# Expert stage of a two-block network: low halves of the weights on VectorE, all dense gates through DRAM, own buffers for the gathered rows

## The chip, the core and the metric

The kernel runs on one core of one Trainium2 chip. The metric is the device time of one execution in microseconds. Three timed runs of the kernel before gave 3890.19, 3895.22 and 3896.65 us; their median, 3895.22 us, is the number to beat or to match.

## The reference, cut to what matters

A DiT-like two-layer network is followed by a second block (gated delta rule beside a linear recurrence, attention over a memory) and, as its last part, a product-key expert layer on 512 tokens of 1024 features. The change touches only that last part:

```python
def peer_ffn(h, wq, subkeys, u_tab, v_tab):      # u_tab, v_tab: 16384 experts x 1024
    q = (t @ wq).reshape(ntok, 8, 2, 128)         # 8 heads, two half keys
    sc = einsum('thpd,hpkd->thpk', q, subkeys)    # 128 sub-keys for each half
    s1, i1 = top_k(sc[:, :, 0], 16)
    s2, i2 = top_k(sc[:, :, 1], 16)
    cand = s1[..., :, None] + s2[..., None, :]
    best, pos = top_k(cand.reshape(ntok, 8, 256), 16)
    idx = e1 * 128 + e2                           # place of an expert in the 128 x 128 grid
    gate = softmax(best, axis=-1)
    # for each token: 8 x 16 experts
    act = gelu(einsum('phkd,pd->phk', u_tab[ib], tb)) * gb
    return einsum('phk,phkd->pd', act, v_tab[ib])
```

The output is the RMS-normalised sum of the stream and this layer, in float32.

## The kernel before, in words

Matrix products take float32 operands as a sum of two parts in the fast float32 format: a high half and a low half (the rest). `mm3` (L274) forms each product from three matmuls: high by high, high by low, low by high. `weight` (L264) loads a weight tile of 128 x 1024 (512 KB) into a buffer `wr`, lets ScalarE write the high half `wh` (L245) and another engine write the low half `wl` by a subtraction (L253). That engine is GpSimd, except where the call says `'dve'`.

The expert layer (`peer`, L1384) treats its four tiles of 128 tokens in two ways. Three tiles ("dense") go through all 16384 experts in 128 blocks: `hidden(b)` (L1418) multiplies block b of the u table (8 products of three matmuls, 128 x 384 outputs, `H`), applies gelu (`Hg`); `operand` (L1463) multiplies the result with the gates of that block and splits it into `ach` and `acl`; then 18 matmuls of 512 columns (L1541) add its product with block b of the v table to six PSUM banks `acc`, which stay for all 128 blocks. The fourth tile ("fetched") reads only the experts that its tokens chose: 128 steps `up` (an indirect DMA of 128 rows, 512 KB, of the u table, and one VectorE instruction, L1562, that takes their dot products) and 128 steps `down` (the same for the v table; L1573 adds the weighted rows to `y0`). The gathers are issued by GpSimd (L1557). `fetches(n)` puts n further steps into the program; the calls spread them over the blocks.

The layer runs in four stages. (1) Scores and `topk`. (2) `decode` (L1684) turns positions into rows, columns and gates with one-hot tables `oh` of 128 x 1024; `gates` (L1602) expands them to dense gates: for every 4 tokens VectorE and ScalarE write two one-hot tables `o`, TensorE multiplies them into `G`, and ScalarE copies the result to `Gs` (two buffers of 4 MB, for 64 tokens each). Tiles 0 and 1 of the dense ones are then written to DRAM (`dGate`); those of the last tile stay in `Gs`. Meanwhile `hidden` runs for the first 72 blocks, whose results go to DRAM (`dAct`). (3) Blocks 0 to 71: each reads its `Hr` back from `dAct`, and for every two blocks the gates `Gt` from `dGate` (rows of 512 bytes); VectorE multiplies by `Gt` (L1470) and twice by `Gs` (L1473). This stretch is called the head below. (4) Blocks 72 to 127, which compute `hidden` here: the tail. Of the v weights two in three have their low half on GpSimd, one in three on VectorE (L1530); the u weights have theirs on GpSimd.

Weights, gathered rows and some results share the 7 buffers `wr`. The order of each engine's instructions isn't that of the source: the framework's scheduler sets it when the program is built, from a model of each instruction's time and from when buffers come free. Once built, the order is fixed, and each engine takes its instructions in that order; SyncE issues all plain DMAs in order, GpSimd the gathers in order.

## Time and profile before

| | |
|---|---|
| timed runs, us | 3890.19, 3895.22, 3896.65 |
| profiled execution, span first to last instruction, us | 3892.8 |
| busy share of the span | PE 91%, DVE 73%, POOL 52%, ACT 39% |
| first one-hot table of `decode` | 2597 us |
| first dense gates (`Gs`) to the last | 2698 to 2992 us |
| first matmul into `acc` | 3003.7 us |
| end of the head, first product of block 72 | about 3340 us |
| last matmul into `acc` | 3881 us |

The profile has one time for the profiled execution, its span, 2.4 us under the median of the timed runs. In its rows PE is TensorE, PEld its weight loads, DVE VectorE, ACT ScalarE, POOL GpSimd, SP SyncE. Consecutive matmuls overlap in the records, so the distance between their starts, not their duration, is what one costs. PEclk is the clock that TensorE was granted, as a share of full speed. The DMA share is the mean busy share of the 16 DMA engines. All stages before 2597 us are other parts of the network.

### The profile page before, as it was taken

Reading aid. Unit: us, or ns where it says so; the run is one execution under the profiler, and the core shown is the slowest. Engines: PE = TensorE matmul, PEld = TensorE weight load, DVE = VectorE, ACT = ScalarE, POOL = GpSimd, SP = SyncE. Lnnn points to the kernel's source line nnn. Section 1 sums busy time; section 2 is a strip of 40 time slices with the busy share of each in tenths; the row PEclk is TensorE's granted clock in tenths of the full one; section 3 lists DMA queues with packets and bytes.
Section 4 is the critical chain, followed back from the end, with each engine's and each line's share of the span. In section 5 each row is a group of like instructions: output and inputs, shape, how many; then the busy total and the mean of one; then the engine's idle time right before and its main releaser. Section 6 shows DMA issues by size and latency. Waiting matters only on the chain.

```text
span 3892.8 us, 51884 instructions
## 1 busy us (share of the span) xinstructions
PE 3539.8 (91%) x18415; PEld 2940.5 (76%) x18415; DVE 2841.6 (73%) x5128; ACT 1536.0 (39%) x2548; POOL 2004.9 (52%) x1230
## 2 busy tenths in 40 slices
PE   6899898999999869999999998997799999989898
PEld 4566666788877767788787976897788777777777
DVE  7895768778779793322486354789998999888874
ACT  4433663332323343322344443343576233322223
POOL 3763105345555553344445432467545676888773
PEclk9999998999999889999999998998999999999999
DMA  5442023344434343223322333245576998888782
GB/s 215 141 145 66 25 69 101 107 131 126 131 99 157 124 182 119 86 93 98 120 76 89 110 116 107 84 139 179 181 248 214 316 319 306 283 284 290 274 285 90
DMA packets 279012, 615.42 MB, mean 158 GB/s; under 512 B 49888, under 2 KB 148832, under 8 KB 275936
## 3 DMA queue, kind: packets, MB, share of 16 engines
q1 hardware_dynamic: 237248, 477.34, 37.3%
q0 software_dynamic: 36864, 134.23, 10.0%
q8 instruction: 145, 2.38, 0.3%
q10 hardware_dynamic: 4640, 0.53, 0.1%
q14 instruction: 115, 0.94, 0.1%
HBM read 539.27 MB, written 72.71 MB: 157 GB/s over the span
## 4 chain that ended last, share of the span: by engine, by line
PE 21%; DVE 9%; POOL 8%; issue 7%; DMA 4%; ACT 1%; POOLq 0%; ACTq 0%; DVEq 0%; SPq 0%
POOL wl L253 4%; POOL wr L1557 3%; PE mm L277 3%; PE mm L279 3%; PE mm L278 3%; DMA wr<-in_p_v_dram,idx 2%; PE H L279 2%; PE H L278 2%; PE H L277 2%; DVE o L1617 1%; PE acc L279 1%; PE acc L277 1%; PE acc L278 1%; PE G L1620 1%; DVE wr L1562 1%
## 5 line engine op out<-in xcount | busy, mean ns | idle before, releaser
L253 POOL TENSOR_TENSOR wl<-wr,wh 128x1024 fp32r<-128x1024 f32 x469 | 1168.7, 2495 | 1043.3 <-ACT wh L245 975.2
L245 ACT ACTIVATE wh<-wr 128x1024 fp32r<-128x1024 f32 x512 | 536.2, 1053 | 690.7 <-PE mm L278 352.4
L277 PE MATMUL mm<-hh,wh 128*128 128x512 f32 (+1 forms) x1024 | 365.6, 363 | 17.7 <-ACT hh L340 8.0
L279 PE MATMUL H<-wh,wl 128*128 128x384 f32 x1024 | 352.8, 344 | 18.8 <-POOL wl L253 17.6
L278 PE MATMUL mm<-hl,wh 128*128 128x512 f32 (+1 forms) x1024 | 366.8, 359 | 0.1
L279 PE MATMUL mm<-hh,wl 128*128 128x512 f32 (+1 forms) x1024 | 363.9, 356 | 0.9 <-POOL wl L253 0.8
L277 PE MATMUL H<-wh,wh 128*128 128x384 f32 x1024 | 348.9, 341 | 1.5 <-ACT Hg L1425 1.5
L278 PE MATMUL H<-wl,wh 128*128 128x384 f32 x1024 | 349.5, 341 | 0.0
L277 PE MATMUL acc<-wh,ach 128*128 128x512 f32 x768 | 310.0, 404 | 26.4 <-ACT ach L245 24.9
L279 PE MATMUL acc<-wh,acl 128*128 128x512 f32 x768 | 308.9, 406 | 19.1 <-DVE acl L253 19.0
L278 PE MATMUL acc<-wl,ach 128*128 128x512 f32 x768 | 306.8, 399 | 0.0
L277 PE MATMUL mm<-fh,wh 128*128 128x512 f32 (+1 forms) x768 | 276.6, 361 | 2.2 <-DVE x L531 2.2
L278 PE MATMUL mm<-fl,wh 128*128 128x512 f32 (+1 forms) x768 | 275.9, 360 | 2.4 <-DVE fl L253 2.4
L279 PE MATMUL mm<-fh,wl 128*128 128x512 f32 (+1 forms) x768 | 274.8, 359 | 0.0
L1573 DVE SCALAR_TENSOR_TENSOR y<-wr,wgt,y 128x1024 f32<-128x1024 f32 x127 | 230.0, 1811 | 50.3 <-DMA wr<-in_p_v_dram,idx 49.8
L277 PEld LDWEIGHTS mm<-hh,wh 128*128 128x128 f32 x1024 | 197.9, 194 | 52.6 <-ACT hh L340 9.2
L1562 DVE SCALAR_TENSOR_TENSOR wr<-wr,tt 128x1024 f32<-128x1024 f32 x128 | 206.0, 1616 | 40.8 <-DMA wr<-in_p_u_dram,idx 23.4
L279 PEld LDWEIGHTS mm<-hh,wl 128*128 128x128 f32 x1024 | 197.8, 193 | 29.5 <-POOL wl L253 1.7
L278 PEld LDWEIGHTS mm<-hl,wh 128*128 128x128 f32 x1024 | 198.4, 194 | 28.1 <-issue 0.9
L1557 POOL DMA_INDIRECT wr<-in_p_u_dram,idx x128 | 162.4, 1269 | 107.3 <-DVE wr L1562 48.5
L279 PEld LDWEIGHTS H<-wh,wl 128*128 128x128 f32 x1024 | 195.1, 191 | 29.1 <-POOL wl L253 28.7
L1557 POOL DMA_INDIRECT wr<-in_p_v_dram,idx x128 | 167.9, 1312 | 93.6 <-DVE y L1573 46.2
(809 smaller groups left out, 8754.5 us busy)
## 6 DMA issues: line engine op xcount, KB each, us to landing
wr<-in_mlp_w_dram SPq DMA_DIRECT2D x128, 512.0 KB
wr<-in_p_ut_dram SPq DMA_DIRECT2D x128, 512.0 KB
wr<-in_p_v_dram SPq DMA_DIRECT2D x128, 512.0 KB
aw<-in_ada_w_dram SPq DMA_DIRECT2D x48, 512.0 KB
wr<-in_ada_w_dram SPq DMA_DIRECT2D x32, 512.0 KB
dGate<-Gs SPq DMA_DIRECT2D x32, 512.0 KB
Gt<-dGate SPq DMA_DIRECT2D x64, 256.0 KB
dAct<-Hg SPq DMA_DIRECT2D x72, 192.0 KB
```

The lines of the kernel that those rows point to most:

```text
L245: self.nc.scalar.activation(dst, src, AF.Copy, **({} if scale is None else {'scale': scale}))
L253: e.tensor_tensor(dst, src, hi.bitcast(F32), op=OP.subtract)
L277: mm(out, ah, bh, start=first, stop=False)
L278: mm(out, ah, bl, start=False, stop=False)
L279: mm(out, al, bh, start=False, stop=last)
L1557: gp.indirect_dma_start(out=r, out_offset=None, in_=tab, in_offset=bass.IndirectOffsetOnAxis(ap=idx[:, s:s + 1], axis=0))
L1562: v.scalar_tensor_tensor(r, r, 1.0, tt, op0=OP.mult, op1=OP.mult, accum_out=dots[:, s:s + 1])
L1573: v.scalar_tensor_tensor(y0, r, wgt[:, s:s + 1], y0, op0=OP.mult, op1=OP.add)
L1617: v.tensor_scalar(o1[:, t], iota, row, gate, op0=OP.is_equal, op1=OP.mult)
L1620: nc.tensor.matmul(p[:, t * 128:(t + 1) * 128], o2[:, t], o1[:, t], start=True, stop=True)
```

## The change

The low halves: `weight` takes its engine from a new field, `'pool'` at first and `'dve'` from the end of `topk` on, so that all 256 weight tiles of stages 2 to 4 have their low half on VectorE; so has the multiplication of the one-hot tables in `decode`. The gates: all three dense tiles are written to DRAM, read back four blocks at a time (rows of 1 KB, 768 KB for each read), and one VectorE instruction multiplies a whole block. The 8 MB of `Gs` are given back after stage 2. The gathered rows: in stages 3 and 4 they have 9 buffers of their own (`rw`), and the 7 `wr` are left to the weights.

```diff
+        self.lo_eng = 'pool'
...
-    def weight(self, ap, lo_eng='pool'):
+    def weight(self, ap, lo_eng=None):
+        lo_eng = lo_eng or self.lo_eng
...
+            self.rp, self.rb_ = self.wp, ('wr', self.wb[0])
...
-            dG = tc.dram_tile([ND - 1, 2, 128, 128, 64], F32, name='dGate')
+            dG = tc.dram_tile([ND, 2, 128, 128, 64], F32, name='dGate')
...
-            G2 = [self.t(gp_, [128, 128, 64], f'Gs{i}') for i in range(2)]
             with ExitStack() as e1:
+                G2p = e1.enter_context(self.pool('pgs'))
+                G2 = [self.t(G2p, [128, 128, 64], f'Gs{i}') for i in range(2)]
...
+                self.lo_eng = 'dve'
...
-                        if j < ND - 1:
-                            for a in range(0, 128, 16):
-                                nc.sync.dma_start(dG[j, i, :, a:a + 16], G2[i][:, a:a + 16])
+                        for a in range(0, 128, 16):
+                            nc.sync.dma_start(dG[j, i, :, a:a + 16], G2[i][:, a:a + 16])
...
+                self.rp, self.rb_ = e1.enter_context(self.pool('rows')), ('rw', 9)
...
-                    if b % 2 == 0:
-                        G = self.t(tp, [128, 2 * (ND - 1), 2, 64], 'Gt', bufs=2)
-                        nc.sync.dma_start(G, dG[:, :, :, b:b + 2].rearrange('j i e a t -> e (j i) a t'))
+                    if b % 4 == 0:
+                        G = self.t(tp, [128, 2 * ND, 4, 64], 'Gt', bufs=2)
+                        nc.sync.dma_start(G, dG[:, :, :, b:b + 4].rearrange('j i e a t -> e (j i) a t'))
...
-                    Hm = H[:, :M].rearrange('e (j t) -> e j t', t=64)
-                    v.tensor_tensor(Hm, Hm, Gt[-1][:, :, b % 2], op=OP.mult)
-                    for i in range(2):
-                        ts = slice(M + 64 * i, M + 64 * i + 64)
-                        v.tensor_tensor(H[:, ts], H[:, ts], G2[i][:, b], op=OP.mult)
+                    Hm = H.rearrange('e (j t) -> e j t', t=64)
+                    v.tensor_tensor(Hm, Hm, Gt[-1][:, :, b % 4], op=OP.mult)
...
-                    wv = self.weight(I['p_v'][b * 128:(b + 1) * 128], 'pool' if b % 3 else 'dve')
+                    wv = self.weight(I['p_v'][b * 128:(b + 1) * 128])
...
-            r = self.t(self.wp, [128, D], 'wr', bufs=self.wb[0])
+            r = self.t(self.rp, [128, D], self.rb_[0], bufs=self.rb_[1])
...
-                gp.tensor_tensor(oh.rearrange(...), oh.rearrange(...), atf[:, hs, i, None, :].to_broadcast([128, 4, K, K]), op=OP.mult)
+                v.tensor_tensor(oh.rearrange(...), oh.rearrange(...), atf[:, hs, i, None, :].to_broadcast([128, 4, K, K]), op=OP.mult)
```

The scheduler sets the order of the changed program anew. Three places are shown. In VectorE's order in the head, near block 40, before (`wr,dots` is an `up` step, `acl` the end of a block's operand, `wl` a weight's low half):

```order
L253 TENSOR_TENSOR acl_28377<-Hr_28371,ach_28376 128x384
L1470 TENSOR_TENSOR Hr_28407<-Hr_28407,Gt_28409 128x256
L1473 TENSOR_TENSOR Hr_28407<-Hr_28407,Gs_4366_21345 128x64
L1473 TENSOR_TENSOR Hr_28407<-Hr_28407,Gs_4367_21346 128x64
L1562 SCALAR_TENSOR_TENSOR wr_28546,dots_21343<-wr_28546,tt_21240 128x1024
L1470 TENSOR_TENSOR Hr_28445<-Hr_28445,Gt_28409 128x256
L1473 TENSOR_TENSOR Hr_28445<-Hr_28445,Gs_4366_21345 128x64
L1473 TENSOR_TENSOR Hr_28445<-Hr_28445,Gs_4367_21346 128x64
L253 TENSOR_TENSOR acl_28415<-Hr_28407,ach_28414 128x384
```

The same place now (line numbers are those of the changed file, one or two higher):

```order
L254 TENSOR_TENSOR acl_28336<-Hr_28330,ach_28335 128x384
L1563 SCALAR_TENSOR_TENSOR rw_30417,dots_21343<-rw_30417,tt_21240 128x1024
L254 TENSOR_TENSOR wl_28468<-wr_28465,wh_28467 128x1024
L1563 SCALAR_TENSOR_TENSOR rw_30443,dots_21343<-rw_30443,tt_21240 128x1024
L1563 SCALAR_TENSOR_TENSOR rw_30446,dots_21343<-rw_30446,tt_21240 128x1024
L254 TENSOR_TENSOR wl_28504<-wr_28501,wh_28503 128x1024
L1563 SCALAR_TENSOR_TENSOR rw_30488,dots_21343<-rw_30488,tt_21240 128x1024
L1474 TENSOR_TENSOR Hr_28366<-Hr_28366,Gt_28332 128x384
L1563 SCALAR_TENSOR_TENSOR rw_30514,dots_21343<-rw_30514,tt_21240 128x1024
L254 TENSOR_TENSOR acl_28370<-Hr_28366,ach_28369 128x384
```

Where one fetched step stood beside a block, three or so stand now. Over the whole order, of the 256 fetched steps 36 stood in stage 2, 81 in the head and 139 in the tail before; now 33 stand in stage 2, 217 in the head and 6 in the tail. VectorE's order in the tail, near block 100, before:

```order
L253 TENSOR_TENSOR acl_31731<-Hg_31717,ach_31730 128x384
L1573 SCALAR_TENSOR_TENSOR y_4333_21241<-wr_31870,wgt_21344,y_4333_21241 128x1024
L1573 SCALAR_TENSOR_TENSOR y_4333_21241<-wr_31900,wgt_21344,y_4333_21241 128x1024
L1562 SCALAR_TENSOR_TENSOR wr_31942,dots_21343<-wr_31942,tt_21240 128x1024
L1562 SCALAR_TENSOR_TENSOR wr_31945,dots_21343<-wr_31945,tt_21240 128x1024
L253 TENSOR_TENSOR wl_31906<-wr_31903,wh_31905 128x1024
L1470 TENSOR_TENSOR Hg_31792<-Hg_31792,Gt_31725 128x256
```

And there now:

```order
L254 TENSOR_TENSOR acl_31429<-Hg_31419,ach_31428 128x384
L254 TENSOR_TENSOR wl_31535<-wr_31532,wh_31534 128x1024
L254 TENSOR_TENSOR wl_31600<-wr_31597,wh_31599 128x1024
L1474 TENSOR_TENSOR Hg_31490<-Hg_31490,Gt_31498 128x384
L254 TENSOR_TENSOR acl_31502<-Hg_31490,ach_31501 128x384
L254 TENSOR_TENSOR wl_31606<-wr_31603,wh_31605 128x1024
```

The fetched steps are gone from the tail, and both low halves of each block have come. The third place is TensorE's order at the end of stage 2 (`G` are the products of the gates, `x4` for four tokens). Before, matmuls of `hidden` stood between the last groups and after them:

```order
L277 MATMUL H_26694<-wh_21323,wh_26690 128x384
L1620 MATMUL G_24304<-o_5017_24305,o_5018_24306 128x128 x4
L278 MATMUL H_26694<-wl_21324,wh_26690 128x384
L279 MATMUL H_26694<-wh_21323,wl_26691 128x384
L277 MATMUL H_26728<-wh_21274,wh_26724 128x384
```

Now the last 23 groups, 92 products, follow each other with nothing between, and the sums begin right behind:

```order
L1621 MATMUL G_24273<-o_5008_24274,o_5009_24275 128x128 x4
L1621 MATMUL G_24287<-o_5011_24288,o_5012_24289 128x128 x4
L1621 MATMUL G_24301<-o_5014_24302,o_5015_24303 128x128 x4
L1621 MATMUL G_24315<-o_5017_24316,o_5018_24317 128x128 x4
L279 MATMUL acc_26901<-wh_26922,ach_26916 128x512
```

All 72 blocks of `hidden` thus stand before the last 23 groups of gates. On SyncE the 16 writes of the last tile's gates stand ahead of the first reads of `Hr` and `Gt`; on VectorE 19 low halves stand among the last instructions of `topk`, 57 between there and the last gates, 72 in the head and 108 in the tail. Of the one-hot multiplications 16 came to VectorE.

## Rows read from the trace of the kernel before

**Rows 1.** Busy time by stretch: start:end, length, engines, granted clock, DMA share, GB/s.

```profile
2597.00:3003.00 406.00, 342.68 (x2117) 330.28 (x2116) 374.25 (x561) 236.18 (x413) 233.39 (x110) 0.95 0.57 193
3003.00:3340.00 337.00, 319.92 (x1362) 252.44 (x1361) 311.21 (x422) 108.78 (x150) 230.15 (x130) 0.98 0.90 310
3340.00:3880.00 540.00, 495.19 (x2369) 424.05 (x2369) 419.45 (x455) 163.73 (x234) 403.70 (x228) 0.99 0.73 252
3880.00:3893.00 13.00, 0.94 (x5) 0.41 (x3) 7.54 (x18) 3.71 (x10) 0.00 (x0) 0.70 0.33 122
```

**Rows 2.** Waits in the tail, 3340 to 3880: total, times, longest.

```profile
PEld H L279 <- POOL wl L253: 25.3, 29, 2.2
```

**Rows 3.** TensorE's instructions in time, two dense stretches: start, duration.

```profile
3602.00 0.33 PE L279 MATMUL H<-wh,wl 128*128 128x384 f32 x1
...
3605.12 0.34 PE L279 MATMUL H<-wh,wl 128*128 128x384 f32 x1
3605.29 0.40 PE L277 MATMUL acc<-wh,ach 128*128 128x512 f32 x1
...
3609.26 0.39 PE L279 MATMUL acc<-wh,acl 128*128 128x512 f32 x1
```

**Rows 4.** VectorE's instructions in time, tail.

```profile
3604.07 1.27 DVE L1573 SCALAR_TENSOR_TENSOR y<-wr,wgt,y 128x1024 f32<-128x1024 f32 x1
3605.26 0.55 DVE L253 TENSOR_TENSOR acl<-Hg,ach 128x384 fp32r<-128x384 f32 x1
...
3619.93 5.26 DVE L1573 SCALAR_TENSOR_TENSOR y<-wr,wgt,y 128x1024 f32<-128x1024 f32 x1 [2.66 <-DMA wr<-in_p_v_dram,idx]
...
3634.17 1.21 DVE L253 TENSOR_TENSOR wl<-wr,wh 128x1024 fp32r<-128x1024 f32 x1
...
3642.25 1.22 DVE L1562 SCALAR_TENSOR_TENSOR wr<-wr,tt 128x1024 f32<-128x1024 f32 x1
```

**Rows 5.** GpSimd's instructions in time, tail.

```profile
3616.12 1.95 POOL L1557 DMA_INDIRECT wr<-in_p_v_dram,idx  x1 [0.30 <-issue]
3618.38 0.94 POOL L1557 DMA_INDIRECT wr<-in_p_v_dram,idx  x1 [0.30 <-issue]
3619.34 4.75 POOL L253 TENSOR_TENSOR wl<-wr,wh 128x1024 fp32r<-128x1024 f32 x2
```

**Rows 6.** DMA queues in the head, 3003 to 3340: packets, MB, share of 16 engines.

```profile
q1 hardware_dynamic: 40383, 61.49, 54.1%
q0 software_dynamic: 11761, 42.85, 35.7%
```

**Rows 7.** Two slices of 10 us with the DMA engines full, columns as in Rows 1.

```profile
2870.00:2880.00 10.00, 9.91 (x67) 9.29 (x65) 10.00 (x15) 7.42 (x16) 6.20 (x3) 1.00 1.03 414
3400.00:3410.00 10.00, 8.81 (x45) 7.67 (x43) 7.64 (x4) 1.50 (x3) 9.23 (x6) 1.00 1.00 376
```

**Rows 8.** Groups of instructions, 2597 to 3003: busy, mean ns, idle before them, releasers.

```profile
L253 POOL TENSOR_TENSOR wl<-wr,wh 128x1024 fp32r<-128x1024 f32 x54 | 139.6, 2589 | 99.7 <-ACT wh L245 92.1 <-DVE o L1612 6.1 <-PE G L1620 1.3
L1621 ACT ACTIVATE Gs<-G 128x512 f32<-128x512 f32 x96 | 100.1, 1090 | 3.4 <-PE G L1620 3.4
L1619 ACT ACTIVATE o<-o,ct 128x128 f32<-128x128 f32 x192 | 65.8, 393 | 85.7 <-DVE o L1613 85.4
```

**Rows 9.** VectorE's instructions in time, stage 2.

```profile
2598.38 0.21 DVE L1697 CAST k_f<-k_pi 128x128 f32<-128x128 uint32 x1
...
2694.77 0.68 DVE L1612 TENSOR_TENSOR o<-c_iota,ct 128x512 f32<-128x512 f32 x1
...
2696.22 0.68 DVE L1612 TENSOR_TENSOR o<-c_iota,ct 128x512 f32<-128x512 f32 x1
```

**Rows 10.** A group of instructions at the end of the top-k, 2440 to 2640.

```profile
L1644 DVE MAX8 k_best<-k_c 128x8 f32<-128x112 f32 x32 | 8.9, 278 | 19.1 <-POOL k_c L1679 18.9
```

**Rows 11.** TensorE's instructions in time, stage 2, after an idle stretch.

```profile
2778.76 1.62 PE L1620 MATMUL G<-o,o 128*128 128x128 f32 x8 [2.93 <-DVE o L1617]
...
2780.82 0.52 PE L278 MATMUL H<-wl,wh 128*128 128x384 f32 x1
```

More of the change, by code (lines that the diff above doesn't have):

```diff
@@ L1463, in operand @@
                 def operand(b, H):
-                    if b % 2 == 0:
-                        G = self.t(tp, [128, 2 * (ND - 1), 2, 64], 'Gt', bufs=2)
-                        nc.sync.dma_start(G, dG[:, :, :, b:b + 2].rearrange('j i e a t -> e (j i) a t'))
+                    if b % 4 == 0:
+                        G = self.t(tp, [128, 2 * ND, 4, 64], 'Gt', bufs=2)
+                        nc.sync.dma_start(G, dG[:, :, :, b:b + 4].rearrange('j i e a t -> e (j i) a t'))
                         Gt.append(G)
-                    M = 128 * (ND - 1)
-                    Hm = H[:, :M].rearrange('e (j t) -> e j t', t=64)
-                    v.tensor_tensor(Hm, Hm, Gt[-1][:, :, b % 2], op=OP.mult)
-                    for i in range(2):
-                        ts = slice(M + 64 * i, M + 64 * i + 64)
-                        v.tensor_tensor(H[:, ts], H[:, ts], G2[i][:, b], op=OP.mult)
+                    Hm = H.rearrange('e (j t) -> e j t', t=64)
+                    v.tensor_tensor(Hm, Hm, Gt[-1][:, :, b % 4], op=OP.mult)
                     return self.split(tp, [128, N], 'ac', H, bufs=3)
@@ L1711, in decode @@
                 v.tensor_tensor(oh, a[:, hs].rearrange('p h k -> p (h k)')[:, :, None].to_broadcast([128, 4 * K, K]), iota[:, None, :K].to_broadcast([128, 4 * K, K]), op=OP.is_equal)
-                gp.tensor_tensor(oh.rearrange('p (h k) a -> p h k a', h=4), oh.rearrange('p (h k) a -> p h k a', h=4), atf[:, hs, i, None, :].to_broadcast([128, 4, K, K]), op=OP.mult)
+                v.tensor_tensor(oh.rearrange('p (h k) a -> p h k a', h=4), oh.rearrange('p (h k) a -> p h k a', h=4), atf[:, hs, i, None, :].to_broadcast([128, 4, K, K]), op=OP.mult)
                 v.tensor_reduce(e[:, 64 * hh:64 * hh + 64], oh, axis=AX.X, op=OP.add)
```

## The prediction, made before the changed kernel ran

> **What bounds the kernel now.** I read the busy times by stretch first, then the waits, then single instructions in time. Everything before 2597 us is untouched, so only three stretches count [rows 1]. In stage 2 (2597 to 3003) VectorE is the busiest, 374 of 406 us, and TensorE idles for 63. In the head (3003 to 3340) two things are full at once: TensorE is busy for 320 of 337 us, and the 16 DMA engines for 90% at 310 GB/s. In the tail TensorE is busy for 495 of 540 us, and the DMA engines for 73% at 252 GB/s; its waits name GpSimd's low halves [rows 2].
>
> What TensorE needs when nothing holds it up is read from starts, not durations: 18 steps from 3602.00 to 3605.12 give 0.1733 us for a matmul of `hidden`, 17 steps from 3605.29 to 3609.26 give 0.2335 us for one into `acc` [rows 3]. A block is 24 x 0.1733 = 4.16 us and 18 x 0.2335 = 4.20 us. The head thus needs 72 x 4.20 = 303 us of its 337 (and some 15 for residuals and the first blocks of `hidden`); the 55 blocks of the tail need 55 x 8.36 = 460 of 540. So 80 us of waits lie in the tail, under 20 in the head.
>
> VectorE's rows show why it is so busy: a `down` step takes 1.27 us at 3604, but 5.26 us at 3619.93, while GpSimd ran two low halves of 4.75 us together from 3619.34 [rows 4, 5]. VectorE stands still for as long as GpSimd subtracts.
>
> **Stage 2, part by part.** The low half costs 1.21 us on VectorE [rows 4] and 2.59 on GpSimd here [rows 8], and on GpSimd it stops VectorE too. The sum on VectorE from the first one-hot to the last gates, by the counts of the new order: 96 gate groups x 1.45 us (two starts, [rows 9]) = 139; 57 low halves x 1.21 = 69; 32 one-hot tables, of the same 1024 elements as a low half, x 1.21 = 39; 33 fetched steps x 1.25 = 41; 16 reductions of such tables, taken as 1.21, 19; some 60 small ones, taken as the 0.21 of a cast [rows 9], 13. Together 320 us. With the counts of before (no low halves, 16 tables, 36 steps) the same prices give 235, and 374 was measured: the 139 us between them are the 139.6 us of GpSimd's 54 low halves [rows 8]. So the stalls go, and 85 us of work comes for 139 of stalls.
>
> The start moves little: 19 low halves come into the top-k, 23 us, while VectorE's 18.9 us of waiting for GpSimd's candidate sums [rows 10], which stood behind low halves, go. I take 2600 us, between 2597 and 2620. VectorE idled for 32 us in this stretch, waiting for gathers and tables; I keep 15 of them, between none and all. The last 23 groups have no `hidden` beside them, so they go at ScalarE's pace of 1.09 + 2 x 0.39 = 1.87 us [rows 8] instead of 1.45, 10 us more, and TensorE has nothing else to do. Last gates: 2600 + 320 + 15 + 10 = 2945 us, where it was 2992; bounds 2917 and 2992. What is late next is the DRAM trip: block 0 needs the last 4.2 MB of gates written, on SyncE's queue ahead of the reads of `Hr` and `Gt`: 11 us at 376 GB/s [rows 7], so the head begins at 2956 (it was 3003).
>
> **The head.** Here the order decides. Own buffers and a free GpSimd let the scheduler put 217 fetched steps between the first and the last block of the head, where there were 81; the tail keeps 6 of its 139. VectorE takes them in order, and a block's low half and operand stand behind them, so TensorE can't run ahead of the gathers. Four floors for the 72 blocks:
> - TensorE: 303 us, and some 15 as before.
> - VectorE: 121 `down` x 1.27 + 96 `up` x 1.22 + 72 low halves x 1.21 + 72 multiplies and 72 `acl` x 0.55 (a multiply of 384 columns taken as an `acl`) = 154 + 117 + 87 + 79 = 437 us [rows 4].
> - GpSimd: 217 gathers between 1.24 and 2.25 us (0.30 us ahead of each, and 0.94 to 1.95 for it, [rows 5]) = 269 to 488 us.
> - DMA engines: the gathers took 35.7% of 337 us, 120 us for 42.85 MB, or 82 of 0.524 MB: 1.47 us each. The plain DMAs took 54.1%, 182 us [rows 6]. Now 217 x 1.47 + 182 = 502 us with all engines always full. The gates' reads grow from 2 to 3 parts in bytes, and their rows from 512 to 1024 bytes, so fewer packets: I add nothing, between -20 and +14.
>
> The DMA floor is the highest. Windows with the engines full show a share of 1.00 to 1.03 [rows 7], the whole stretch 0.90 [rows 1]; with 9 gathers and 7 weights in flight I take 0.98, so 512 us, between 490 and 558. By bytes it is the same: 104.5 MB of before, 135 gathers more (71 MB), 4.7 MB more of gates, 180 MB in all, need 479 us at the 376 GB/s of the mixed slice. TensorE idles for some 190 us here.
>
> The edit of the multiply (three instructions into one) and the four-block reads cost or save nothing on the path: VectorE is under the DMA floor by 75 us, which covers both.
>
> **The tail** becomes TensorE's: both low halves, 2 x 1.21, and 2 x 0.55 of operand are 3.5 us of VectorE in a block of 8.36, and nothing fetched stands ahead of them. Its DMA traffic is 1.25 MB a block, 149 GB/s. TensorE has 56 blocks into `acc` left and 54 of `hidden` (two stand in the head): 235 + 225 = 460 us. Then 13 us for the last norm and the output [rows 1].
>
> Sum: 2956 + 512 + 460 + 13 = 3941 us of span, against 3892.8 of the profiled execution; the median of the timed runs lies 2.4 us above that span, so 3943 us. The tail gains 80 us and stage 2 gains 47, and the head loses 175: fetched work that lay under a half-idle DMA system in the tail is crowded into the stretch where it was already full.
>
> **The rivals.**
> *The DMA engines carry more.* One slice moved 414 GB/s [rows 7], with long rows and few gathers. At that rate 180 MB take 435 us, VectorE's 437 bound the head, and the span is 2956 + 437 + 460 + 13 = 3866, so 3868: faster. It decides from a head of 464 us down, 388 GB/s held throughout. For it: nothing in the rows is a hard ceiling. Against: the slices with gathers give 376 at most. Chance 15%.
> The Trainium skill (DMA: Bandwidth & Descriptors, section Bandwidth) gives 425 GB/s for one large transfer and about 358 GB/s as what memory yields a core; an estimate by the first is 424 us for the head's bytes, under VectorE's floor, by the second 503. The trace's full slices, 376 and 414, lie between the two.
>
> *TensorE falls to half clock in the head.* After an idle stretch of 2.93 us its matmuls of `hidden` took 0.52 us instead of 0.33 [rows 11, 3], that is 1.2 GHz for a while. With 40% idle this can recur. All of the head at 1.2 GHz would be 72 x 8.4 = 605 us and 4036 in all; it only decides if two thirds of the head run so, since below that TensorE still fits into 512. Chance 8%.
>
> *GpSimd can't issue fast enough* because VectorE is never still now. At 2.25 us a gather it is 488 us, hidden; with a wait for one more VectorE instruction of 1.27 us each, 217 x 3.52 = 764 us, 4195 in all. The rows show no gather instruction beyond 1.95. Chance 5%.
> The Trainium skill (SBUF — State Buffer, section SBUF: two separate sides) warns of this: while VectorE holds the port that it shares with GpSimd, GpSimd can't write descriptors. The 0.94 to 1.95 us of such instructions in this trace agree with short waits of that kind, no longer ones.
>
> *No difference*: a head of about 464 us, or gates earlier and a head near 490. Chance 7%.
>
> **How the numbers follow.** The forecast, a head bound by its transfers, has the other 65%: 3943 us, by its bounds about 3900 to 3990. Faster by over 0.2% (about 8 us, what a measurement of this kernel can tell from none) 15%, within that 7%, slower 78%. The range from 3885 to 4005 holds the forecast, the no-change case and the upper edge of the first rival.
>
> **What would show it.** In the profile of the changed kernel: last gates near 2945 and no VectorE instruction of 1024 elements above 2 us for GpSimd's sake; a head of about 510 us with a DMA share above 0.95 and TensorE busy for 60%, waiting for VectorE's `acl` or `wl`, and VectorE for gathers; then a tail of 460 us with TensorE at nearly 100% and half the DMA traffic. Wrong if the head takes under 465 us, if its DMA share stays under 0.9 while VectorE is full, or if the last gates come near 2990.

## The result, and the profile after

The changed kernel takes 3934.55 us (3927.95 to 3938.68, four runs), the kernel before 3895.93 (3890.19 to 3899.7) beside it: a ratio of 1.01, 95% interval 1.0085 to 1.0114. It is slower by 39 us; the prediction said 3943, and slower. The span of its profiled execution is 3925.8 us.

The busy times by stretch of the changed kernel, with the columns of [rows 1]; stage 2, the wait for the gates, the head, the tail and the end:

```profile
2590.00:2937.00 347.00, 333.91 (x2164) 329.17 (x2162) 320.15 (x665) 246.40 (x422) 51.43 (x36) 1.00 0.69 240
2937.00:2964.00 27.00, 0.05 (x1) 0.05 (x1) 0.63 (x2) 0.52 (x1) 8.44 (x9) 0.50 0.96 355
2964.00:3447.00 483.00, 361.20 (x1368) 280.22 (x1369) 414.78 (x535) 113.27 (x151) 277.98 (x213) 0.88 0.99 372
3447.00:3914.00 467.00, 467.00 (x2336) 420.31 (x2335) 199.82 (x235) 169.18 (x227) 0.00 (x0) 1.00 0.44 137
3914.00:3926.00 12.00, 0.67 (x3) 0.19 (x1) 7.54 (x18) 3.45 (x10) 0.00 (x0) 0.72 0.36 132
```

Against [rows 1]: stage 2 is shorter by some 58 us and the tail by 73, and the head is longer by 146, with its DMA engines busy nearly throughout (share 0.99, where it was 0.90) and TensorE busy for 361 of 483 us; 27 us in which only GpSimd works, at its gathers, are new. In the tail the DMA share fell from 0.73 to 0.44 and GpSimd does nothing: the gathers that used to lie there are in the head. The DMA queues of the head (packets, MB, share of 16 engines), to be held against [rows 6]:

```profile
q0 software_dynamic: 30890, 112.44, 60.7%
q1 hardware_dynamic: 35900, 67.03, 38.4%
```

The gathers' queue carries 112.44 MB for 42.85. The waits of the head show who stands behind it (engine and line waiting, for whom, total us, times, longest):

```profile
ACT wh L246 <- PE acc L281: 215.3, 69, 8.3
PEld acc L279 <- ACT ach L246: 167.2, 38, 31.3
PE acc L279 <- ACT ach L246: 151.1, 37, 31.1
ACT ach L246 <- DVE Hr L1474: 125.8, 44, 5.4
POOL rw L1558 <- DVE y L1574: 95.8, 64, 8.4
```

TensorE waits for the operand, the operand for its multiply on VectorE, the multiply stands behind fetched steps, and GpSimd waits for VectorE to free a row. VectorE's own groups in the head say what it waits for (busy us, mean ns, idle us before them, what ended that):

```profile
L1574 DVE SCALAR_TENSOR_TENSOR y<-rw,wgt,y 128x1024 f32<-128x1024 f32 x121 | 155.1, 1282 | 1.5
L1563 DVE SCALAR_TENSOR_TENSOR rw<-rw,tt 128x1024 f32<-128x1024 f32 x96 | 114.7, 1219 | 0.0
L254 DVE TENSOR_TENSOR wl<-wr,wh 128x1024 fp32r<-128x1024 f32 x72 | 88.3, 1226 | 58.3 <-ACT wh L246 57.7
```

It stands for 1.5 us ahead of its 217 fetched steps: each row had landed 3.6 us or more before its step, 9.2 in the median. It waits for ScalarE's high halves, and ScalarE for TensorE: 67 of its 68 longer waits ahead of a high half end within 0.25 us of a block's last product, and the weights had landed 21 us or more before. One stall of TensorE, from three engines' rows:

```profile
3211.01 1.56 PE L281 MATMUL acc<-wh,acl 128*128 128x512 f32 x6
3212.66 1.06 ACT L246 ACTIVATE wh<-wr 128x1024 fp32r<-128x1024 f32 x1 [3.18 <-PE acc L281]
3213.75 1.23 DVE L254 TENSOR_TENSOR wl<-wr,wh 128x1024 fp32r<-128x1024 f32 x1 [0.72 <-ACT wh L246]
...
3217.18 0.56 DVE L1474 TENSOR_TENSOR Hr<-Hr,Gt 128x384 f32<-128x384 f32 x1
...
3217.82 0.52 ACT L246 ACTIVATE ach<-Hr 128x384 fp32r<-128x384 f32 x1 [4.10 <-DVE Hr L1474]
3218.39 0.79 PE L279 MATMUL acc<-wh,ach 128*128 128x512 f32 x1 [5.82 <-ACT ach L246]
```

The last product of a block frees a buffer of high halves; ScalarE fills it; VectorE writes the low half, takes two fetched steps, and only then multiplies for the block that TensorE waits for. This is a ring made by the order, with no transfer in it. VectorE multiplies for a block only after TensorE has ended the block before it in 27 of 71 blocks of this head (before: none). Three things could thus set the head's length: the transfers, the sum of VectorE's work, and this ring. The runs were made to part the first two.

### The profile page after: what moved, and what is told of

Its sections match the earlier page's. It is cut to its first block, busy times and chain, and to the rows that moved or that the text cites. A ratio compares the mean times of both kernels' runs of the same rounds, so it can differ in the third digit from the quotient of the medians.

```text
span 3925.8 us, 51174 instructions
## 1 busy us (share of the span) xinstructions
PE 3537.9 (90%) x18415; PEld 2959.1 (75%) x18415; DVE 2682.0 (68%) x5101; ACT 1551.9 (40%) x2548; POOL 1437.2 (37%) x1001
## 5 line engine op out<-in xcount | busy, mean ns | idle before, releaser
L254 POOL TENSOR_TENSOR wl<-wr,wh 128x1024 fp32r<-128x1024 f32 (+1 forms) x256 | 633.9, 2479 | 860.3 <-ACT wh L246 817.9
L254 DVE TENSOR_TENSOR wl<-wr,wh 128x1024 fp32r<-128x1024 f32 x256 | 312.8, 1222 | 283.3 <-ACT wh L246 282.7
L279 PE MATMUL acc<-wh,ach 128*128 128x512 f32 x768 | 330.1, 430 | 151.1 <-ACT ach L246 151.1
L280 PE MATMUL acc<-wl,ach 128*128 128x512 f32 x768 | 323.6, 421 | 0.0
L279 PEld LDWEIGHTS acc<-wh,ach 128*128 128x128 f32 x768 | 157.3, 205 | 201.5 <-ACT ach L246 167.2
L281 PE MATMUL acc<-wh,acl 128*128 128x512 f32 x768 | 256.6, 400 | 0.0
L1558 POOL DMA_INDIRECT rw<-in_p_v_dram,idx x127 | 162.7, 1281 | 224.7 <-ACT o L1620 86.5
L279 PEld LDWEIGHTS H<-wh,wh 128*128 128x128 f32 x1024 | 193.0, 188 | 4.1 <-ACT wh L246 1.6
L280 PEld LDWEIGHTS H<-wl,wh 128*128 128x128 f32 x1024 | 192.9, 188 | 2.3
```

The source lines that it names most:

```text
L254: e.tensor_tensor(dst, src, hi.bitcast(F32), op=OP.subtract)
L279: mm(out, ah, bh, start=first, stop=False)
L280: mm(out, ah, bl, start=False, stop=False)
L281: mm(out, al, bh, start=False, stop=last)
L1558: gp.indirect_dma_start(out=r, out_offset=None, in_=tab, in_offset=bass.IndirectOffsetOnAxis(ap=idx[:, s:s + 1], axis=0))
```

## The experiments

Theory 1: the loss is the order, 217 gathers crowded into the stretch whose transfers are full. It makes two claims, that the crowded order is the loss (runs 1 and 5) and that the transfers then set the head's length (run 4). Theory 2: VectorE's work in order bounds the head. Theory 3: the low halves on VectorE, or the gates through DRAM, cost by themselves. One table for all runs. The last gates are the start of the last `Gs`; the first and last dense product are the first and last start of a matmul of `ach` by `wh` into `acc`; the end of the head is the start of the 72nd `acl`. Each ratio is to runs of the kernel before that were made beside the run (medians 3892.46 to 3895.93 us).

| kernel | last gates | first dense | end of head | last dense | time, us | ratio to before, interval |
|---|---|---|---|---|---|---|
| before | 2991.0 | 3003.7 | 3337.0 | 3878.9 | 3895.93 | 1 |
| changed | 2932.9 | 2964.0 | 3446.4 | 3912.6 | 3934.55 | 1.01, 1.0085 to 1.0114 |
| 1 shared buffers | 2944.9 | 2969.0 | 3289.2 | 3761.6 | 3776.39 | 0.9695, 0.9678 to 0.9711 |
| 2 low halves only | 2943.3 | 2949.5 | 3273.3 | 3845.9 | 3857.88 | 0.9885, 0.9856 to 0.9914 |
| 3 low halves back | 2947.5 | 2993.5 | 3484.5 | 3957.6 | 3972.91 | 1.0203, 1.0186 to 1.022 |
| 4 light steps | 2915.9 | 2955.1 | 3427.5 | 3893.7 | 3908.81 | 1.0034, 1.0023 to 1.0045 |
| 5 paced | 2934.3 | 2965.6 | 3285.3 | 3757.0 | 3772.37 | 0.969, 0.9674 to 0.9706 |
| 6 shared, gates by two | 2943.5 | 2960.8 | 3282.8 | 3755.8 | 3768.0 | 0.9674, 0.9656 to 0.9691 |
| 7 low halves, gates by four | 2942.4 | 2947.6 | 3275.5 | 3821.3 | 3837.62 | 0.9857, 0.9839 to 0.9875 |
| 8 paced, filled | 2936.8 | 2974.2 | 3294.9 | 3766.6 | 3772.3 | 0.9685, 0.9668 to 0.9703 |
| 9 six shared buffers | 2945.4 | 2963.6 | 3272.1 | 3757.9 | 3774.48 | 0.9694, 0.9674 to 0.9715 |
| 10 low halves, eight buffers | 2942.3 | 2948.6 | 3274.6 | 3840.3 | 3849.36 | 0.9877, 0.9853 to 0.99 |
| 11 paced, gates by two | 2930.7 | 2947.9 | 3267.3 | 3739.2 | 3759.08 | 0.9656, 0.9635 to 0.9676 |
| 12 decode multiply only | 2948.8 | 2977.9 | 3319.4 | 3862.0 | 3877.07 | 0.9958, 0.9942 to 0.9975 |

### 1. Own buffers undone

```diff
-                self.rp, self.rb_ = e1.enter_context(self.pool('rows')), ('rw', 9)
+                pass
```

> The changed kernel, but the gathered rows of dense blocks take the weights' seven buffers again (as in the kernel before). In the order, 72 fetched steps then stand among VectorE's first 72 dense blocks and 139 behind them, against 217 and 6. Theory 1 (the own buffers let 217 gathers crowd into the first 72 blocks, where the transfers are the bound, and leave none for the last 56): first dense product at 2964 as now, 72 blocks in about 330 us as TensorE allows, 56 blocks in about 475, end 13: span 3782, time 3775 to 3820 us. Theory 2 (VectorE's own sum of work sets the first 72 blocks): also faster, about the same time, so this run doesn't tell 1 from 2. Theory 3 (the crowding costs nothing; the loss comes from low halves on VectorE and gates through DRAM, and own buffers are a gain): 3935 us or more.

Measured 3776.39 us. Its head and tail, columns as above:

```profile
2969.00:3290.00 321.00, 311.99 (x1336) 250.02 (x1337) 236.89 (x324) 105.34 (x143) 96.34 (x76) 0.98 0.91 320
3290.00:3763.00 473.00, 473.00 (x2368) 425.91 (x2367) 355.31 (x434) 173.43 (x235) 178.24 (x135) 1.00 0.81 293
```

TensorE is the bound in both. The tail carries its 139 gathers and is only 6 us longer than without them; the head is 162 us shorter. The whole loss, and the gain that it hid, go with the own buffers or with the order that they allow; theory 3 falls in so far as it called them a gain. No multiply of this head starts after the end of the block before, and TensorE's stalls sum to some 20 us.

### 2. The low halves alone

```diff
 (the kernel before, with:)
+                self.lo_eng = 'dve'          # behind the top-k
-                    wv = self.weight(..., 'pool' if b % 3 else 'dve')
+                    wv = self.weight(...)    # low half on VectorE
-                gp.tensor_tensor(oh...)
+                v.tensor_tensor(oh...)       # decode's second multiply
```

> The kernel before with one part of the change: after the top-k the low halves of weights and the multiply of the decode on VectorE; the last tile's gates stay in SBUF with three multiplies a block, gathered rows stay in the weights' buffers. Order: 71 fetched steps among the first 72 dense blocks, 139 in the tail. Theory 1 (this part is a gain by itself): last gates at about 2934 as in the changed kernel (64 us earlier than before), first dense product some 10 us later, 330 us of head, 475 us of tail without GpSimd's stretched low halves, 13 of end: span 3762, time 3755 to 3800 us. Theory 3 (VectorE can't bear the low halves): 3900 us or more. Beside the run with shared buffers it prices the gates through DRAM: theory 1 gives that part about 20 us of loss at the boundary.

Measured 3857.88 us, not 3755 to 3800. Stage 2 and the head came near what was expected (gates 9 us later), the tail took 573 us instead of 475, and 542 in the kernel before. Its waits in the tail, and below them those of run 1 on the same lines:

```profile
ACT ach L246 <- DVE Hg L1476: 297.9, 53, 11.0
POOL wr L1560 <- DVE y L1576: 112.9, 27, 7.3
POOL wr L1560 <- DVE wr L1565: 91.1, 22, 6.8
DVE y L1576 <- DMA wr<-in_p_v_dram,idx: 82.6, 45, 3.9
DVE wr L1565 <- DMA wr<-in_p_u_dram,idx: 63.3, 40, 3.8
```

```profile
POOL wr L1558 <- DVE wl L254: 148.1, 55, 7.0
ACT ach L246 <- DVE Hg L1474: 31.9, 42, 1.4
DVE wr L1563 <- DMA wr<-in_p_u_dram,idx: 9.1, 9, 2.4
```

The boundary costs what was expected: 6 us from the last gates to the first dense product here, 24 in run 1. In the tail VectorE waits 146 us for gathered rows here, and the operand 298 us for its multiply behind them. A gather gets its buffer from a fetched step a few instructions ahead (204 us of such waits on GpSimd), in run 1 from a low half further back. A row is asked for 7.2 us ahead of its step here, 9.7 us there (medians in the tail, start of the k-th gather on GpSimd to the k-th fetched step on VectorE; called the lead below). Runs 6, 7, 9 and 10 ask why.

### 3. The low halves back on GpSimd

```diff
-                self.lo_eng = 'dve'
-                    wv = self.weight(I['p_v'][b * 128:(b + 1) * 128])
+                    wv = self.weight(I['p_v'][b * 128:(b + 1) * 128], 'pool' if b % 3 else 'dve')
```

> The changed kernel with the low halves on GpSimd again (two of three of the value weights, all others), so only the gates through DRAM and the own buffers are left, and the decode's multiply on VectorE. Order: 211 fetched steps among the first 72 dense blocks, 13 behind. Theory 1 (low halves on VectorE are a gain of some 60 us in stage 2; the crowding costs the same as in the changed kernel): first dense product at about 3027, head 480 to 490, tail 475, end 13: span about 4000, time 3985 to 4030 us. Theory 3 (low halves on VectorE are the loss): 3890 us or less.

Measured 3972.91 us: slower than the changed kernel, so the low halves on VectorE are a gain and theory 3 falls. Its head is about as long (491 us, DMA share 0.98), with 211 fetched steps in it: a free GpSimd isn't needed for the crowding. But I had put 60 us of stage 2 on the low halves, and the last gates come only 15 us later here; the first dense product comes 30 us later, with TensorE busy for 36 of the 46 us between. Run 12 follows from that. The tail takes 473 us, TensorE busy throughout, with the low halves on GpSimd and only 13 fetched steps in it.

### 4. VectorE's fetched steps made light

```diff
-            v.scalar_tensor_tensor(r, r, 1.0, tt, ...)
+            v.scalar_tensor_tensor(r[:, :128], r[:, :128], 1.0, tt[:, :128], ...)
-                v.scalar_tensor_tensor(y0, r, wgt[:, s:s + 1], y0, ...)
+                v.scalar_tensor_tensor(y0[:, :128], r[:, :128], wgt[:, s:s + 1], y0[:, :128], ...)
```

> The changed kernel with VectorE's fetched steps on 128 of the 1024 columns of each row (the rest of the row is gathered and not used, so the first tile's output lacks it); every transfer stays. Order as in the changed kernel: 217 fetched steps among the first 72 dense blocks, 6 behind. VectorE's sum in the head falls from 414 us to about 414 - 217 x 1.05 = 186 us. Theory 1 (the head is bound by its transfers, 179 MB at some 372 GB/s = 482 us): the head stays at 465 to 485 us, time 3915 to 3935 us. Theory 2 (VectorE's work in order sets the head): the head falls towards TensorE's 330 us, time 3780 to 3820 us.

Measured 3908.81 us; the head of this kernel:

```profile
2955.00:3428.00 473.00, 361.88 (x1368) 280.86 (x1369) 218.20 (x535) 113.61 (x152) 208.42 (x213) 0.89 1.00 377
```

VectorE's work is halved (218 us for 415), and the head is 10 us shorter, at a DMA share of 1.00. Theory 2 asked for over 100 us, so the sum of VectorE's work doesn't set the head. The length is what theory 1 forecast, but that the transfers set it isn't shown. VectorE's groups in this head:

```profile
L254 DVE TENSOR_TENSOR wl<-wr,wh 128x1024 fp32r<-128x1024 f32 x72 | 88.3, 1226 | 218.8 <-ACT wh L246 174.3 <-issue 39.1 <-DMA Hr<-dAct 3.2
L1574 DVE SCALAR_TENSOR_TENSOR y<-rw,wgt,y 128x128 f32<-128x128 f32 x121 | 42.2, 349 | 1.9
L1563 DVE SCALAR_TENSOR_TENSOR rw<-rw,tt 128x128 f32<-128x128 f32 x96 | 24.0, 286 | 0.0
```

It waits for high halves, not for rows, and the ring is there again: 24 of 71 multiplies start after the end of the block before, and TensorE's waits for `ach`, without the first, are 108 us, for 120 in the changed kernel. The fetched steps make up 43 us of the stalls there and 8 here, but VectorE's waits inside the stalls rise from 12 to 26. So the order, which this run kept, accounts for the length with no transfer in it. A run that keeps the order and takes the gathers out would part the two; none was made. A DMA share near 1 doesn't decide it either: the head of run 11 has 0.98, and there TensorE is busy for 310 of 320 us.

### 5. Own buffers kept, the fetched steps paced

```diff
-                    v.tensor_tensor(Hm, Hm, Gt[-1][:, :, b % 4], op=OP.mult)
+                    self.mul = v.tensor_tensor(Hm, Hm, Gt[-1][:, :, b % 4], op=OP.mult).ins
-                        fetches(more)
+                        with tc.issue_after(self.mul):
+                            fetches(more)
-                    fetches(1.15 if b < NA else more)
+                    with tc.issue_after(self.mul):
+                        fetches(1.15 if b < NA else more)
```

> The changed kernel whole (nine own buffers for gathered rows), but each dense block's fetched steps are queued on VectorE behind the multiply by the gates of the block that the source writes ahead of them; nothing is left out. Order: 83 fetched steps among the first 72 dense blocks, 140 in the tail, against 217 and 6. Theory 1 (the loss lies in where the 217 steps stand and not in the own buffers): first dense product at about 2964, head 320 to 330 as with the shared buffers, tail 474, end 13: span about 3775, time 3765 to 3800 us. Rival (own buffers cost by themselves, since gathers run ahead of the weights and gates on the DMA engines): 3850 us or more.

Measured 3772.37 us. This is the clean test: all parts of the change are there, the edit only moves the steps' place on VectorE's queue (the scheduler then orders the rest anew), and the loss of 39 us becomes a gain of some 120. One multiply of its head starts after the end of the block before. Its tail:

```profile
3286.00:3758.00 472.00, 472.00 (x2363) 425.10 (x2362) 352.47 (x436) 172.43 (x235) 166.51 (x133) 1.00 0.81 287
```

The first claim of theory 1 holds, and in sum the own buffers cost nothing; rows are asked for 24 us ahead here and VectorE waits for none. Beside run 1 they gain nothing either.

### 6 and 7. Two-block and four-block reads exchanged

```diff
 (6: the kernel of run 1, with:)
-                    if b % 4 == 0:
-                        G = self.t(tp, [128, 2 * ND, 4, 64], 'Gt', bufs=2)
+                    if b % 2 == 0:
+                        G = self.t(tp, [128, 2 * ND, 2, 64], 'Gt', bufs=2)
 (7: the kernel of run 2, with the reverse for its two tiles)
```

> The run with the shared buffers, but its gates are read back two blocks at a time as in the kernel before, not four. Order: 73 fetched steps in the head, 138 in the tail; between two gate multiplies of the tail both low halves mostly stand together. The run with the low halves alone had a tail of 574 us against 474 with the shared buffers, with 146 us of VectorE waits for gathered rows that were issued 7 us ahead of their step (there 9.6). Theory A (the two-block reads make that tail): time 3860 to 3880 us. Theory B (the last tile's gates in SBUF, or the order that goes with it, makes it): tail 474 to 480, time 3775 to 3790 us.

> The run with the low halves alone (the last tile's gates in SBUF, three multiplies a block), but the other two tiles' gates are read back four blocks at a time. Order: between two gate multiplies of the tail a fetched step stands ahead of each low half, as in the run with low halves alone. Theory A (two-block reads made that run's tail of 574 us): tail about 475, time 3755 to 3790 us. Theory B (the order that goes with the last tile in SBUF makes it: low halves and multiplies stand behind fetched steps whose rows are late): tail 550 to 580, time 3840 to 3870 us.

Measured 3768.0 and 3837.62 us, tails of 473 and 546 us: theory B, with both times a few us below its ranges. The size of the reads makes at most 27 of the 100 us of the long tail. In run 7 VectorE waits 120 us for rows (lead 6.8 us), in run 6 6 us (lead 9.5).

### 8. The wait for the gates filled

```diff
 (the kernel of run 5, with:)
                 for b in range(NA):
-                    H = hidden(b)
+                    with tc.issue_after(self.lastG) if b >= NA - 5 else ExitStack():
+                        H = hidden(b)
```

> The paced kernel, and the last five of the 72 early hidden products are queued on TensorE behind the last gate product, so that TensorE works while the gates go to DRAM and come back (31 us idle in the changed kernel, 23 with the shared buffers); nothing is left out. Theory 1: the first dense product comes at 2960 to 2968 as before, or a little later, with 21 us of hidden products inside the wait, and stage 2 is shorter by what TensorE and not VectorE set there, 5 to 20 us: time 5 to 20 us below the paced kernel's, 3750 to 3785 us. Rival (stage 2 is set by VectorE alone, and the low halves of those five blocks and their weights' loads delay the gates' return): the same time as the paced kernel or up to 10 us more.

Measured 3772.3 us, the same as run 5: the rival. TensorE has 20 us of work inside the wait now, but the last gates come at 2936.8, no earlier than without it (2934.3), so TensorE didn't set them. The first product comes 9 us later in the profiled execution, which took 3782.26 us and was the longest of the four.

### 9 and 10. One buffer less, one more

```diff
 (9: the kernel of run 1)
-            self.wb = (7, 4, 4)
+            self.wb = (6, 4, 4)
 (10: the kernel of run 2)
-            self.wb = (7, 4, 4)
+            self.wb = (8, 3, 4)
```

> The run with the shared buffers, with six in place of seven for weights and gathered rows. Order: 69 fetched steps in the head, 144 in the tail, and in the tail mostly both low halves or the fetched steps stand together, unlike the run with low halves alone. Theory L (a row that is issued some 7 us ahead of its step comes late, and the multiply and the low halves behind that step come late with it; the tail of 574 us is that): gathers are issued 6.5 to 8 us ahead instead of 9.6, VectorE waits 80 us or more for rows in the tail, tail 510 to 570, time 3810 to 3880 us. Theory P (only the pattern in which a fetched step stands ahead of each low half makes such a tail): waits for rows under 40 us, tail 474 to 490, time 3770 to 3795 us.

> The run with low halves alone, with eight shared buffers in place of seven for weights and gathered rows (and three in place of four for the high halves, since there is no room). Order: 71 fetched steps in the head, 139 in the tail, a fetched step ahead of each low half as in that run. Theory L: gathers are issued 9 us or more ahead of their step instead of 7, VectorE's waits for rows in the tail fall from 146 to under 70 us, tail 480 to 520, time 3760 to 3805 us. Theory P: the tail stays at 550 to 580, time 3835 to 3865 us.

Measured 3774.48 and 3849.36 us, tails of 486 and 566 us. With six buffers the lead fell from 9.7 to 8.2 us and VectorE's waits for rows rose from 16 to 44 us, less than theory L asked for. The tail is 13 us longer by the table, but it begins earlier there: TensorE is busy for 483 of its 486 us, and from the first dense product to the last it is 794 us, for 793 in run 1. With eight buffers the lead didn't rise (6.7 us, waits of 143 us), so run 10 has the same time as run 2 without telling what a longer lead would do. GpSimd's waits for a fetched step's buffer don't mark the slow tails (2, 7, 10): they are 181 to 227 us there, and 188 in run 5, whose own buffers only fetched steps can free. Of the kernels with all low halves on VectorE, the slow tails alone have both a lead of 7.2 us or less and an order in which a fetched step stands right ahead of most low halves, 76 to 78 of 112 or 113. In runs 1, 6 and 9 it does so for 24 to 40 of some 110; in runs 5 and 11 for 49 and 62, but there rows are early, and nothing is lost. So late rows and steps placed ahead of the low halves go together with the long tail. Which of the two makes it isn't shown, and why the scheduler deals the buffers so when the last tile's gates stay in SBUF is open.

### 11. The version that beats both

```diff
 (the kernel of run 5, with the two-block reads of run 6 and:)
-                self.rp, self.rb_ = e1.enter_context(self.pool('rows')), ('rw', 9)
+                self.rp, self.rb_ = e1.enter_context(self.pool('rows')), ('rw', 5)
```

> The paced kernel with two changes at the boundary: gates are read back two blocks at a time, so the first read is half as long, and five own buffers for gathered rows in place of nine, so that five and not nine gathers (2.6 MB for 4.7) run beside that read. Nothing is left out. Theory 1: last gates at 2935, first dense product at 2950 to 2957 instead of 2965.6, head 320, tail 473 (rows still issued 14 us or more ahead): time 3758 to 3768 us, 5 to 15 us below the paced kernel's. Rival (the lead of five buffers is too short in the tail): 3785 us or more.

Measured 3759.08 us, 3.4% under the kernel before. The wait for the gates, the head and the tail:

```profile
2932.00:2948.00 16.00, 0.14 (x1) 0.14 (x1) 1.19 (x3) 0.71 (x2) 0.00 (x0) 0.50 1.00 350
2948.00:3268.00 320.00, 310.04 (x1336) 249.16 (x1337) 248.97 (x334) 108.96 (x144) 100.80 (x82) 0.99 0.98 338
3268.00:3740.00 472.00, 472.00 (x2366) 425.43 (x2365) 352.51 (x436) 171.31 (x233) 172.35 (x137) 1.00 0.84 291
```

The wait fell from 31 to 17 us by TensorE's count. GpSimd issued no gather in it, where the changed kernel issued nine; its five went ahead of the wait, at 2922 to 2928. The two edits can be told apart by other runs: the wait is 24 us in run 1 (no gathers in it, four blocks a read) and 17 in run 6 (no gathers, two blocks). So the gathers cost some 7 us and the longer read 7. The lead in the tail is 12.8 us, below the 14 that I expected, and VectorE waits for no row. The kernel is 13 us faster than that of run 5 and 9 than that of run 6, but the intervals of the ratios overlap, narrowly with run 5.

### 12. The decode's multiply alone

```diff
 (the kernel before, with:)
-                gp.tensor_tensor(oh.rearrange(...), ..., op=OP.mult)
+                v.tensor_tensor(oh.rearrange(...), ..., op=OP.mult)
```

> The kernel before with one line of the change: the decode's second multiply on VectorE, all else as before (low halves on GpSimd, last tile's gates in SBUF, shared buffers). In the run with the low halves back on GpSimd the last gates came at 2948.6 us and not near 2992 as the kernel before has them, so the low halves were not the whole of the stage's gain. Theory D (GpSimd's sixteen decode multiplies, 2.86 us each in a chain of VectorE, GpSimd, VectorE, held the decode of the tiles and with it the gates): last gates at 2944 to 2958 us, the head 334 and the tail 543 as in the kernel before, time 3845 to 3865 us. Rival (the gain came with the other parts, such as the order without the multiplies from SBUF): last gates at 2980 us or later, time 3880 to 3900 us.

Measured 3877.07 us, 17 us under the kernel before, not 30 to 50. The gates did what theory D says. That multiply's group in the kernel before, and then the group that copies the gates in this kernel (duration min, median, max in ns, first and last start):

```profile
L1712 POOL TENSOR_TENSOR k_oh<-k_oh,k_af x16: 2347/2908/3503, 2598.5 to 2801.0; 128x1024 f32<-128x1024 f32 x16
```

```profile
L1621 ACT ACTIVATE Gs<-G x96: 1018/1082/1177, 2667.1 to 2948.8; 128x512 f32<-128x512 f32 x96
```

The gates end 42 us earlier than in the kernel before by this line alone. But TensorE had products of `hidden` left to do until 2978. It had stood for 47 of the 378 us from 2597 to 2975, mostly at gate products whose tables VectorE had not made yet:

```profile
PE G L1620 <- DVE o L1617: 27.7, 20, 3.4
```

With the gates out of the way, that work was late next, and I had not counted it; the head then took 342 us of its own, some 8 more than before.

## Why the prediction came out as it did

**Stage 2.** The sum of 320 us on VectorE measured 310, from the first one-hot to the last gates:

```profile
2600.00:2934.00 334.00, 323.91 (x2106) 319.17 (x2104) 310.28 (x618) 240.28 (x415) 49.97 (x34) 1.00 0.69 241
```

No low half is stretched; this is the group in stage 2, to be held against [rows 4] and [rows 8]:

```profile
L254 DVE TENSOR_TENSOR wl<-wr,wh 128x1024 fp32r<-128x1024 f32 x59 | 71.7, 1215 | 5.5 <-ACT wh L246 5.4
```

The last gates came at 2934, 11 us ahead of the 2945, 10 of them by that sum; its 24 idle us here are close to the 25 that I added for waits and bare groups. The split was wrong, though: I gave the 139 us of stalls to the low halves alone. Summed over VectorE's instructions of stage 2, the time over the median of the same instructions in the changed kernel is 114 us beside GpSimd's low halves and 25 us beside the decode's multiply in the kernel before, and 90 us beside the low halves in run 12. That the whole 139 matched the 139.6 us of GpSimd's low halves was chance. Runs 3 and 12 show that the decode's multiply, taken from GpSimd, moves the gates by 42 us, and the low halves by 15 more. In run 12, with the low halves still on GpSimd, `hidden` isn't done by the time of the last gates; in the changed kernel it is.

**The trip through DRAM.** Predicted 11 us, measured 30. This term was furthest off for its size: I priced the writes and not what queues behind and beside them. VectorE's first multiply:

```profile
DVE Hr L1474 <- DMA Gt<-dGate: 31.7, 1, 31.7
```

The 27 us from 2937 on moved 9.6 MB at 355 GB/s: 5.6 MB of plain DMAs (the rest of the writes, then the first reads of gates, of `Hr` and of residuals), and 4.0 MB of the nine gathers into the new buffers. In run 11, with two-block reads and five buffers, 5.6 MB and no gather move in that time, and the wait falls to 17.

**The head.** Predicted 512 us, measured 483. The size came near, and the reason isn't borne out. The step was that the DMA engines, with 9 gathers and 7 weights in flight, bound the head. On average 3.4 gathers and 1.1 weights were in flight (issue to landing), and of the signs that I named, VectorE waiting for gathers didn't come (1.5 us in all); TensorE was busy for 75% and not 60. What held TensorE up is the ring: 120 us of waits for `ach`. And behind each stall its products start 0.43 us apart for a while, for 0.23, at the lower of its clock's two levels, 1.2 GHz (granted 0.52 from 2964 to 2967, behind the longest idle stretch): 42 us more in the head, where run 1 has 7. From the first product into `acc` to that of block 72 the head is 488 us, in run 1 332; stalls make 120 of these 156 us and the clock 36. That bytes and rate gave nearly the same length is luck as far as the runs show.

In the sum's own terms, the mis-sized one is the gather: 60.7% of 483 us for 112.44 MB, 214 gathers of 0.524 MB, is 1.37 us each, where [rows 6] gave 1.47. The plain DMAs came at 185 us for 182, the share at 0.99 for 0.98, the bytes at 179.75 MB for 180. VectorE was busy for 415 us, for 437.

**The tail and the end.** 467 us for 460, TensorE at 100%, DMA at 137 GB/s for 149; 12 us for 13. The errors offset: stage 2 -11, the trip +19, the head -29, the tail +7, the end -1, in all -15 on a span of 3941. The 7 us of the tail lie in where it is cut: from the first product into `acc` of block 72, where the sum's 56 and 54 blocks begin, to the last one it is 460 us, as predicted, and the head is 24 short and not 29. Run 3 shows that the low halves needn't have left GpSimd for that tail once the fetched steps were gone.

**The rivals.** That the DMA engines carry more: the head held 372 GB/s, for 351 in the forecast (180 MB in 512 us), and stayed below the 388 that decides. Since no engine waited for rows, 372 isn't shown to be a limit. The page DMA: Bandwidth & Descriptors (Bandwidth) of the Trainium skill, cited ahead, gives 425 and about 358 GB/s; the 372 and 377 measured over 470 us and more lie between. The half clock came for a part of the head (granted clock 0.88 on average). I had let it count only if TensorE filled the head, but the 122 us in which TensorE stood weren't to spare: they are the ring's, and the slower products came on top. GpSimd issued a gather in 1.28 and 1.30 us:

```profile
L1558 POOL DMA_INDIRECT rw<-in_p_v_dram,idx x127 | 162.7, 1281 | 224.7 <-ACT o L1620 86.5 <-DVE y L1574 57.2 <-issue 41.1
L1558 POOL DMA_INDIRECT rw<-in_p_u_dram,idx x96 | 124.6, 1298 | 92.7 <-DVE y L1574 38.6 <-DVE rw L1563 34.6 <-issue 12.5
```

It was no bound.

**What the reasoning got right for the right reason** is that the crowding is the loss: runs 1 and 5 undo it in two ways, and both take the head from 483 to 320 us. It was also right that a block's low half and operand stand behind fetched steps in VectorE's order; but those steps didn't wait for rows. What it said of the cause, own buffers and a free GpSimd, holds for the buffers; run 3 shows the second isn't needed.

## What to carry to other kernels

Buffers of their own let a scheduler pull work forward as far as they reach; look in the new order at where that work lands, and what then stands ahead of the instruction that the busiest engine waits for, before counting the freed waits. Before calling a stretch bound by its transfers, find an engine that waits for a landing; a DMA share near 1 isn't that. Where one stretch is crowded with movable steps and the next half empty, tie these steps to a place in the order rather than take the buffers away. Price a trip through memory with everything that the same change lets loose beside it.

## What was not expected of the hardware

One core's DMA engines held 372 GB/s for 483 us (377 in run 4), over 60% of it in gathers of 4 KB rows, and 400 GB/s for a slice:

```profile
3000.00:3020.00 20.00, 14.14 (x58) 11.31 (x59) 17.31 (x32) 4.15 (x6) 12.34 (x10) 0.87 1.04 400
```

These are rates that were held, not limits. And VectorE's halt beside GpSimd strikes whatever stands there: in the tail of run 3, with GpSimd's low halves and hardly a fetched step, the 384-column multiply took 2476 ns in the median, for 551 in the changed kernel (the 36 long ones overlap a subtraction on GpSimd, the 20 short ones none):

```profile
L1473 DVE TENSOR_TENSOR Hg<-Hg,Gt x56: 550/2476/2765, 3482.9 to 3951.8; 128x384 f32<-128x384 f32 x56
```
